# New durations in the table of a build-time instruction scheduler, and a price for a change of rows on TensorE

## The chip, the cores and the metric

The kernel runs on one core of one Trainium2 chip. The metric is the device time of one execution in microseconds, the median of several runs. A core has a matrix engine (TensorE, PE in the profile, with its weight loads shown apart as PEld), VectorE (DVE), ScalarE (ACT), GpSimd (POOL) and the DMA queues, here issued by SyncE (SP). Each engine works through its own instructions in the order in which the program lists them; across engines they wait on semaphores.

## What is computed

Four transformer layers on 256 tokens of width 1024, all in float32, cut here to their skeleton:

```python
for l in range(2):                       # first block
    x = x + 0.5 * rmsnorm(swiglu(rmsnorm(x, g), w_gate, w_up, w_down), g_post)   # ffn1
    x = x + rmsnorm(token_mixing(rmsnorm(x, g), ...), g_post)                    # mix
    x = x + 0.5 * rmsnorm(swiglu(rmsnorm(x, g), ...), g_post)                    # ffn2
for l in range(2):                       # second block
    x = x + merged(nsa_attention, gated_linear_attention, memory_attention) @ w_out   # hyb
    x = x + square(relu(rmsnorm(x, g) @ w_up)) @ w_down                              # mlp
```

`token_mixing` runs three kinds of attention over 16 heads. `merged` gates and adds three branches: sparse attention (8 heads of 64, in pairs), gated linear attention (4 heads, "gla") and attention into a memory of 256 tokens (4 heads).

## The kernel before

**Main stream.** All weights (some 640 blocks of 128 x 1024 float32, called halves) are read in the order of use. Each is split into a high and a low part in TensorE's faster float32 format: ACT copies the high part (`splits`), DVE subtracts to get the low part (`lows`), and where DVE falls behind, POOL does that subtraction in four pieces of 256 columns (`pooled`). TensorE multiplies each half with all 256 tokens, mostly with 256 or 512 moving columns a matmul (`ws_mm`, `ts_mm`, `ts_bank`). At the end of a stage `finish` multiplies the last chunks, and for each of the two tiles of tokens `residual`, `norm` and `turn_half` make the next stage's input on ACT, DVE and POOL; `turn_half` transposes it on TensorE. In the gaps after the first block's stages TensorE has other products to make (`fill`: keys and values of the memory); `ws_first` starts the next stage with the tile that is ready.

**Background.** The attentions run as tasks beside the main stream. The order of the matmuls inside a task is written out: `scores` and `nsa_pair` give for each segment of scores one matmul over all 128 rows of the array (both parts of one operand stacked) and then one over the 64 rows of the head; `gla` gives for each head a group of some ten products over 64 rows, of 16 to 256 columns, whose operands three multiplications on POOL have prepared (of 128, 256 and 512 columns); before its transposes `nsa_pair` scales probabilities with six instructions on POOL for each of two groups of heads.

**The order.** The program is made by a list scheduler that runs when the kernel is built (`Sched`). Every instruction is an `Op` with a planned duration: `mm` and `tr` set it for TensorE, `Engine` for the other engines. `Sched.run` takes at each step the instruction that can start first by the planner's clocks (`when`), with small biases by priority, and issues it; `matmul` and `stream` advance TensorE's clock. Nothing else of the plan reaches the chip: it sets the order on each engine and which buffer each task gets. Priority 0 (`CHAIN`) is the work at the end of a stage, 2 and 4 are background, 9 is the main stream. A background matmul is held back on purpose:

```python
if t.op.eng == "pe" and 0 < p < 9:
    w = max(w, t.op.rdy + self.SLACK)        # SLACK = 1.17 us
k = (w + t.bias, p, t.seq)                   # main stream: bias 0.05
```

The planner's prices before, in microseconds: a matmul 0.4167e-3 a column plus 0.002; a transpose of 128 columns 0.1067 plus 0.002; a two-operand instruction on POOL 2.07e-3 a column plus 0.157; on POOL a scaling by a column (`tensor_scalar`) 0.85e-3 a column plus 0.24.

Of the kernel before, what the change touches and what calls it, by code (L numbers as in the profile page):

```python
# [45 lines left out]
# ---------------------------------------------------------------- weights  # L46
# The main stream reads the weights in the order of use, in "halves":
# [128, 1024] float32, what one step multiplies with all 256 tokens.

def ws_half(w, c0):  # L50
    """Columns c0:c0+128 of a [1024, n] matrix: [128 p, 8 k, 128 c]."""
    return w[:, c0:c0 + 128].reshape(8, 128, 128).transpose(1, 0, 2).reshape(128, 1024)


def ts_halves(w, cols, per=2):
    """Columns of a [1024, n] matrix, per row chunks of 128 in a half: [128 p, per, n]."""
    a = w[:, cols]
    n = a.shape[1]
    a = a.reshape(8 // per, per, 128, n).transpose(0, 2, 1, 3).reshape(8 // per, 128, per * n)
    if per * n < 1024:  # L60
        a = np.concatenate([a, np.zeros((8 // per, 128, 1024 - per * n), np.float32)], -1)
    return list(a)
# [59 lines left out]
def merge_order(b):  # L122
    """Gates (None, j) and branch halves (i, None) of a branch."""
    if b == 0:
        return [(None, j) for j in range(8)] + [(i, None) for i in range(4)]
    return [u for i in range(4) for u in ((None, 2 * i), (None, 2 * i + 1), (i, None))]
# [56 lines left out]
# ---------------------------------------------------------------- constants of the shapes  # L183
# [9 lines left out]
def constants():  # L193
# [25 lines left out]
    # decay sums: E[tok] = sum over a range of tokens, as columns of 0 or -1/16  # L219
# [10 lines left out]
    # order F, 1, 2, 4, B, 64, 32, 16, 8  # L230

    # predicates for A^T[j, i] of the levels that are computed whole: i = j, and 1, 2, 4, 8
# [13 lines left out]
def prepare(inp, stages):  # L246
# [15 lines left out]
    # block two: per-partition columns of gains, and rows that are broadcast  # L262
# [13 lines left out]
# ---------------------------------------------------------------- the kernel  # L276

class Slots:
    """Tiles that are handed out and returned; a task yields (slots) or (slots, n) to get some."""
# [23 lines left out]
class Op:  # L303
    """One instruction, not yet issued."""
    __slots__ = ("eng", "call", "args", "kw", "cost", "tail", "outs", "ins", "tab", "rdy", "stamp", "fn", "load",
                 "passes", "cols", "dep", "name")

    def __init__(self, eng, call, args, kw, cost, outs, ins, tail=0.0, tab=None, fn=None, load=0.0, passes=1, cols=0.0):
# [5 lines left out]
        self.fn = fn  # L314


def region(a):
    """(name, in PSUM, partitions, elements of a partition) that an operand covers; whole banks of PSUM."""
# [28 lines left out]
class Engine:  # L347
    """Makes the instructions of one engine."""
# [4 lines left out]
    def __getattr__(self, fn):  # L353
# [3 lines left out]
        def make(*args, **kw):  # L357
# [22 lines left out]
            else:  # L380
                k, b = 2.07, 0.157
# [25 lines left out]
class Sched:  # L407
    """Lists the instructions of all tasks in one order: the one that can start first by the engines'
    clocks is issued first. A task is a generator of instructions (Op), of conditions to wait for
    (a function) and of requests for tiles (Slots, or (Slots, n))."""  # L410


    def __init__(self):
# [3 lines left out]
        self.table = None  # L417
# [12 lines left out]
    def step(self, t):  # L430
        """Runs a task up to its next instruction, or until it has to wait."""
# [54 lines left out]
    def stream(self, s, cost, cols):  # L486
        """The end of a matmul that starts at s: the array runs at half its clock in a period that follows
        one of little activity."""
# [9 lines left out]

    def matmul(self, op):
        w = self.ready(op)  # L500
        for i in range(op.passes):
            ld = max(self.loader, w) + op.load
            self.loader = max(ld, self.t.get("pe", 0.0) + 0.002)
# [5 lines left out]
    def when(self, op):  # L509
        c = self.t.get(op.eng, 0.0)  # L510
        if op.eng == "pe":
            return max(c, max(self.loader, self.ready(op)) + op.load)
# [96 lines left out]
class Prog:  # L609
# [41 lines left out]
    # ---- small helpers  # L651
# [10 lines left out]
    def mm(self, out, lhsT, rhs, start, stop, **kw):  # L662
# [3 lines left out]
                  wide * 0.4167e-3 * n, [out], [lhsT, rhs], fn="mm", load=0.836e-3 * m, passes=wide,  # L666
                  cols=wide * n * rhs.shape[0] / 128)

    def tr(self, out, in_, k=128):
        i = self.ident[:k, :k]  # L670
        return Op("pe", self.nc.tensor.transpose, (out, in_, i), {}, 0.8333e-3 * k, [out], [in_, i], fn="tr", load=0.107, cols=2 * k)

    def mm3(self, out, l, r, start=True, stop=True):
        """Product of split operands: l(hl), r(hl) give the parts."""
# [6 lines left out]
    def gain(self, ap):  # L681
        """A gain [1024] on every partition, in a scratch tile."""
# [8 lines left out]
    def hl_gain(self, H, L, src, g):  # L691
        """Split of src * g, g a column or a number."""
# [3 lines left out]
    def chunk(self, src):  # L696
        """A split [128, 256] operand for the main stream."""
# [4 lines left out]
    # ---- weights: loaded and split ahead of the main stream  # L702
# [45 lines left out]
    def pooled(self, low):  # L748
        """Takes what the vector engine falls behind with."""
# [22 lines left out]
    # ---- norms  # L772
    def rstd(self, st, a, b, n):
        """(sum of columns a and b of st + n eps)^-0.5, in place of a."""
# [5 lines left out]
    def norm(self, t, x, Gn, dst, st):  # L780
        """dst[:, k, t, hl, :] = rms(x) * gain of token tile t, transposed and split. Gn: the gain times 32."""
# [31 lines left out]
    # ---- matrix products of the main stream  # L813
    def ws_mm(self, p, w, act, nk=8, off=0, parts=1):
        """Weights stationary. One part: [128 columns, 256]; two, which value() adds: [128 columns, t, hl, 128]."""
# [19 lines left out]
    def ws_first(self, n, done):  # L835
        """The first n products of a stage: those of the first tile of tokens ahead of the others."""
# [23 lines left out]
    def ws_unit(self, parts=1):  # L860
        """One product of the main stream: (result, where it goes back to, parts)."""
# [6 lines left out]
    def value(self, pr):  # L868
        """A product as one [128, 256] operand, and the tile that holds it if there is one."""
# [19 lines left out]
    def ts_bank(self, y, w, c, t, first, last, **kw):  # L889
        """y += tokens of tile t times a chunk w(hl) of weights; c: [128, t, hl, 128]."""  # L890
# [3 lines left out]
    def ts_mm(self, y, w, c, t, first):  # L894
        """y [128, 2, 512] += tokens of tile t times w [128, 1024]."""
# [4 lines left out]
    def ts_group(self, width, split=False):  # L900
        """All tokens times a group of columns: a pair of banks, tokens of a tile in each."""
# [22 lines left out]
    # ---- the end of a stage: the last chunks, residual, next norm  # L924
    def gains(self, post, after):
        """The gains for the end of a stage: that of its result, times 32 and the residual's factor, and the next one's, times 32."""
# [9 lines left out]
    def finish(self, chunks, names, ys, post, after, fills):  # L936
        """The last chunks (by name) of a stage; ys: the banks of the tiles of tokens."""
# [63 lines left out]
    def give_gain(self, name):  # L1001
        """Both tiles of tokens are through with a gain."""
# [5 lines left out]
    # ---- memory: keys and values of both layers, in the gaps between the stages  # L1008
# [16 lines left out]
    def fill(self, f):  # L1025
        """256 columns of the memory's keys (f%4 < 2) or values."""
# [22 lines left out]
    def mem_keys(self, l, c, p, y):  # L1049
        """Normed keys of two heads, transposed: memk[:, head, memory token]."""  # L1050
# [17 lines left out]
    # ---- the feed-forward networks  # L1068
# [71 lines left out]
    # ---- token mixing of block one  # L1140
# [15 lines left out]
    def table(self, name):  # L1156
        """The functions of the next stage, once this one's are done with."""
# [3 lines left out]
    def qk_post(self, l, it, pr, qk):  # L1161
# [9 lines left out]
        else:  # L1171
            # of each of two heads: queries with the high parts on its rows and the low ones on the others;
            # keys with the high parts on all rows, and the low ones on its own
# [55 lines left out]
    def scores(self, s, q, k, rows, stacked, strict=False):  # L1229
        """s: a bank [128 q, (q1: 256 keys | q0: 256 keys)] for each of two row groups."""  # L1230
# [14 lines left out]
    def smax(self, Pt, s, biases):  # L1245
        """Exponentials of biased scores of two maps: P [128, 2, 384], and their sums in st[:, :, 2:4]."""
# [15 lines left out]
    def pv_t(self, Tt, Ps):  # L1262
        """Transposed probabilities [128 k, n, (k0: q0 q1 | k1: q1)] of maps [128 q, (q1: k0 k1 | q0: k0)]."""
# [14 lines left out]
    def pv_mm(self, p, T, col):  # L1278
        """o^T [128 = 2 heads x 64, 256 tokens]; V columns col, col+64."""
# [38 lines left out]
    def att_b(self, j, q, k):  # L1318
# [33 lines left out]
        # r = (mean of the squares of a head + eps)^-0.5 on every partition of the head  # L1352
# [42 lines left out]
    # ---- block two  # L1395
# [31 lines left out]
    def rope_tables(self):  # L1427
        nc, a = self.nc, self.a
        # cos and sin of position * frequency: [128, 3, 8] (two token tiles, block ends)
# [24 lines left out]
    def again(self, tag, shape, dt=FT):  # L1454
        """A new tile in the place of the last one of a tag."""
# [7 lines left out]
    def rope(self, x, cos, sin, shape):  # L1463
        """Rotates the first 16 of the last axis of x [.., 64] in place."""
# [18 lines left out]
    def head_norm(self, x, p, nt, nh, d, gs, times=1.0):  # L1483
        """x [p, nt, nh, d] in place: rms over d, gains (view of x, gain) or none, times a factor."""
# [59 lines left out]
    def cmp_post(self, v, pr):  # L1544
        """The windows of compressed keys or values: 2 x 16 positions of each, split."""
# [55 lines left out]
    def hyb(self, l, after, fills):  # L1601
# [7 lines left out]
        # gates, low-rank gate, memory queries, gla values  # L1609
# [27 lines left out]
        # merge  # L1637
# [39 lines left out]
    # ---- memory attention  # L1677
# [60 lines left out]
    # ---- gated linear attention  # L1738
    def gla_gate(self, l):
        """sp = -log sigmoid of the gates, per token, split: [128 tokens, hl, t, 256]."""  # L1740
# [27 lines left out]
    def gla(self):  # L1768
        nc, gq, gr, gv = self.nc, self.gq, self.gr, self.tB
        och = self.och[1] = {}  # L1770
        for half in range(2):
# [6 lines left out]
            for t in range(2):  # L1778
# [14 lines left out]
                # slots: t0: 1 2 4 B | 64 32 16 8, t1: F 1 2 4 | 64 32 16 8  # L1793
# [36 lines left out]
            # o [tokens, dv] of both heads, normed, then transposed  # L1830
# [41 lines left out]
    # ---- nsa: queries, keys, then the three branches  # L1872
    def nsa_qk(self):
# [17 lines left out]
        # of a row group g: rows 64g.. the high parts, the other rows the low parts  # L1891
# [31 lines left out]
    def split_v(self):  # L1923
        yield lambda: ("o", 1) in self.done
        # a token tile, kind: 64 values of the first group, zeros, 64 of the second
# [7 lines left out]
    def keys(self, src, view):  # L1933
        """The high parts of the keys of a row group on all rows, and the low parts on its own."""
# [261 lines left out]
```

## Time and profile before

| What | Value |
|---|---|
| median of 3 runs | 2043.14 us (2041.13 to 2045.71) |
| span of the profiled execution, first to last instruction | 2040.8 us |
| its own time beside the span | not recorded; the three runs lie 0.3 to 4.9 us above the span |
| mean granted TensorE clock over the span | 0.994 of full speed |
| TensorE: busy in matmuls | 1995.6 us, 98% of the span |
| VectorE, ScalarE, GpSimd busy | 70%, 59%, 13% |

The span is what the profile measured between the first and the last instruction of one execution; start and end of the program lie around it. All instructions of this kernel are recorded at one line, so groups are told apart by tiles and shapes. A matmul's recorded duration overlaps with that of the next, so that the distance of starts tells more than the duration.

### The profile page before, as it was taken

The page shows a single profiled execution, that of the slowest core. Times are in us where ns is not written, and L with a number is a line of the kernel's source. Part 1 is how long each engine was busy: PE and PEld are TensorE (multiplying, and loading weights), DVE is VectorE, ACT ScalarE, POOL GpSimd, SP SyncE. Part 2 cuts the span into 40 slices and gives each one's busy share as a digit, 9 for nine tenths or more (in the row PEclk, how much of TensorE's full clock was granted, in tenths as well). Part 3 has the DMA queues.
Part 4 walks back from the last instruction along what each step waited for, and adds up shares of the span by engine and source line. Part 5 has one row for each costly group of instructions (what it writes and reads, how often), then busy time and mean ns, then how long its engine had stood idle before and what let it go on. Part 6 is the DMA issues. An engine that isn't in the chain of part 4 may idle for free. (4 is left out here: it accounts for less than half of the span.)

```text
span 2040.8 us, 31877 instructions
## 1 busy us (share of the span) xinstructions
PE 1995.6 (98%) x11942; PEld 1732.3 (85%) x11942; DVE 1424.7 (70%) x2525; ACT 1205.0 (59%) x2328; POOL 267.7 (13%) x311
## 2 busy tenths in 40 slices
PE   8999999999999999999999999999999999999999
PEld 7888777888888887788889888998888978898887
DVE  6666887666776678776668777666667787667665
ACT  6655775655565568665556656655555656655553
POOL 1000302000200030020003132310001232411000
PEclk9999999999999999999999999999999999999999
DMA  6655344655665644455565544355565544335553
GB/s 218 222 192 199 117 152 146 215 193 188 208 198 192 206 156 135 167 176 190 187 206 193 173 146 135 102 167 183 192 198 189 165 148 142 114 130 191 188 194 124
DMA packets 100561, 353.77 MB, mean 173 GB/s; under 512 B 12435, under 2 KB 13493, under 8 KB 100406
## 3 DMA queue, kind: packets, MB, share of 16 engines
q1 hardware_dynamic: 100406, 351.74, 52.2%
q8 instruction: 93, 1.52, 0.3%
q14 instruction: 62, 0.51, 0.1%
HBM read 350.64 MB, written 1.05 MB: 172 GB/s over the span
## 5 line engine op out<-in xcount | busy, mean ns | idle before, releaser
L546 PE MATMUL m<-hT,hl 128*128 128x256 f32 (+1 forms) x5856 | 976.4, 322 | 7.7 <-DVE hT L546 7.0
L546 PEld LDWEIGHTS m<-hT,hl 128*128 128x128 f32 x5856 | 853.6, 189 | 104.1 <-DVE hT L546 9.6
L546 ACT CAST hl<-raw 128x1024 fp32r<-128x1024 f32 (+1 forms) x690 | 671.4, 982 | 380.3 <-PE b L546 141.3
L546 DVE TENSOR_TENSOR hl<-raw,hl 128x1024 fp32r<-128x1024 f32 (+1 forms) x641 | 755.5, 1184 | 200.1 <-ACT hl L546 193.1
L546 PE MATMUL b<-hl,chunk 128*128 128x512 f32 x2208 | 517.0, 390 | 0.0
L546 PEld LDWEIGHTS b<-hl,chunk 128*128 128x128 f32 x2208 | 408.9, 188 | 81.8 <-issue 0.7
L546 DVE TENSOR_TENSOR mid<-m,lo 128x256 f32<-128x256 f32 x256 | 108.5, 424 | 221.8 <-ACT lo L546 221.3
L546 PE MATMUL b<-hl,hT 128*128 128x512 f32 (+2 forms) x672 | 149.4, 371 | 0.5 <-DVE hT L546 0.5
L546 ACT CAST chunk<-mid 128x256 fp32r<-128x256 f32 x152 | 61.7, 406 | 120.8 <-DVE mid L546 120.4
L546 POOL TENSOR_SCALAR scr<-scr 128x1024 f32<-128x1024 f32 x17 | 21.1, 1239 | 834.9 <-DMA scr<-ffn_post_g 451.6
L546 PEld LDWEIGHTS b<-hl,hT 128*128 128x128 f32 x672 | 115.9, 188 | 16.6 <-DVE hT L546 0.8
L546 POOL TENSOR_TENSOR hl<-raw,hl 128x256 fp32r<-128x256 f32 x104 | 103.0, 1017 | 192.0 <-ACT hl L546 155.1
L546 ACT COPY lo<-m 128x256 f32<-128x256 f32 x256 | 95.0, 371 | 23.8 <-PE m L546 22.7
L546 PE MATMUL b<-ident,scr 128*128 128x128 f32 (+2 forms) x458 | 78.3, 284 | 17.8 <-DVE scr L546 14.0
L546 PE MATMUL m<-chunk,hl 128*128 128x256 f32 x576 | 82.4, 292 | 0.0
L546 PEld LDWEIGHTS b<-ident,scr 128*128 128x128 f32 (+2 forms) x458 | 54.3, 143 | 33.0 <-DVE scr L546 20.3
L546 PEld LDWEIGHTS m<-chunk,hl 128*128 128x128 f32 x576 | 74.3, 195 | 3.0 <-ACT scr L546 0.7
L546 ACT ACTIVATE scr<-scr,sts 128x16 f32<-128x16 f32 (+2 forms) x152 | 62.8, 415 | 9.4 <-DVE sts L546 9.1
L546 DVE TENSOR_TENSOR chunk<-mid,chunk 128x256 fp32r<-128x256 f32 x152 | 65.3, 430 | 2.3 <-ACT chunk L546 2.0
L546 POOL TENSOR_SCALAR scr<-scr,sts 128x128 f32<-128x128 f32 (+2 forms) x96 | 55.9, 602 | 79.3 <-DVE sts L546 52.1
L546 ACT COPY scr<-b 16x16 f32<-16x16 f32 (+6 forms) x148 | 35.4, 239 | 41.2 <-PE b L546 33.5
L546 ACT ACTIVATE mid<-mid 128x256 f32<-128x256 f32 x88 | 36.7, 417 | 34.1 <-DVE mid L546 34.1
(204 smaller groups left out, 1622.4 us busy)
## 6 DMA issues: line engine op xcount, KB each, us to landing
raw<-w SPq DMA_DIRECT2D x636, 512.0 KB, 3.4
scr<-mem SPq DMA_DIRECT2D x4, 512.0 KB, 6.2
scr<-ffn_post_g SPq DMA_DIRECT2D x4, 512.0 KB, 5.0
bias<-bias SPq DMA_DIRECT2D x6, 256.0 KB, 3.6
scr<-ffn_pre_g SPq DMA_DIRECT2D x3, 512.0 KB, 5.9
scr<-mem_norm SPq DMA_DIRECT2D x2, 512.0 KB, 4.9
scr<-mix_pre_g SPq DMA_DIRECT2D x2, 512.0 KB, 4.2
bias<-alibi SPq DMA_DIRECT2D x4, 256.0 KB, 4.3
```

Source lines behind the costliest of these rows:

```text
L546: r = op.call(*op.args, **op.kw) if op.call is not None else None
```

## The change

TensorE's prices become 0.4227e-3 a column plus 0.0105 for each matmul, 0.011 more for each weight load, and 0.098 for a transpose. The two-operand price of POOL becomes 3.1e-3 a column. Each matmul now has a mode, the number of rows of the array that it uses; in the plan a change of mode costs 0.195 us. While TensorE is in a mode of fewer than 128 rows, `when` moves every matmul of another mode 0.195 us later, so that one of the same mode goes first if it is ready by then. Transposes of 64 rows or fewer take whatever mode is current. SLACK, the biases, the prices of ACT and DVE, of the powers and the scalings on POOL, and the instructions themselves stay. The diff also removes comments and docstrings, left out here.

```diff
+                 mode=None):
...
-        self.fn = fn
+        self.fn, self.mode = fn, mode
...
-                k, b = 2.07, 0.157
+                k, b = 3.1, 0.157
...
-        self.table = None
+        self.table = self.mode = None
...
+    SWITCH = 0.195
+    STEP = 0.0105
+
     def matmul(self, op):
         w = self.ready(op)
+        if op.mode != self.mode:
+            if self.mode is not None:
+                w = max(w, self.t.get("pe", 0.0) + self.SWITCH - op.load)
+            self.mode = op.mode
         for i in range(op.passes):
             ld = max(self.loader, w) + op.load
-            self.loader = max(ld, self.t.get("pe", 0.0) + 0.002)
+            self.loader = max(ld, self.t.get("pe", 0.0) + self.STEP)
...
         if op.eng == "pe":
-            return max(c, max(self.loader, self.ready(op)) + op.load)
+            back = self.SWITCH if self.mode not in (None, 128) and op.mode != self.mode else 0.0
+            return max(c + back, max(self.loader, self.ready(op)) + op.load)
...
-                  wide * 0.4167e-3 * n, [out], [lhsT, rhs], fn="mm", load=0.836e-3 * m, passes=wide,
-                  cols=wide * n * rhs.shape[0] / 128)
+                  wide * 0.4227e-3 * n, [out], [lhsT, rhs], fn="mm", load=0.836e-3 * m + 0.011, passes=wide,
+                  cols=wide * n * rhs.shape[0] / 128, mode=rhs.shape[0])
...
-        return Op("pe", self.nc.tensor.transpose, (out, in_, i), {}, 0.8333e-3 * k, [out], [in_, i], fn="tr", load=0.107, cols=2 * k)
+        return Op("pe", self.nc.tensor.transpose, (out, in_, i), {}, 0.098, [out], [in_, i], fn="tr", load=0.109, cols=2 * k,
+                  mode=128 if k > 64 else self.sch.mode)
```

## Rows read from the trace of the kernel before

**Rows 1.** The page: the span, and each engine's busy time.
```profile
span 2040.8 us, 31877 instructions
PE 1995.6 (98%) x11942; PEld 1732.3 (85%) x11942; DVE 1424.7 (70%) x2525; ACT 1205.0 (59%) x2328; POOL 267.7 (13%) x311
```

**Rows 2.** TensorE's waits: for whom, us in total, times, longest us.
```profile
PE b L546 <- DVE scr L546: 14.0, 21, 1.7
PE b L546 <- POOL scr L546: 10.7, 6, 3.5
PE m L546 <- DVE hT L546: 7.0, 10, 1.0
...
PE b L546 <- DVE chunk L546: 1.0, 1, 1.0
```

**Rows 3.** Groups of matmuls by shape: count, busy us, mean ns, idle before.
```profile
L546 PE MATMUL m<-hT,hl 128*128 128x256 f32 x3936 | 552.0, 286 | 7.7 <-DVE hT L546 7.0 <-DVE scr L546 0.5
L546 PE MATMUL b<-hl,chunk 128*128 128x512 f32 x2208 | 517.0, 390 | 0.0
...
L546 PE MATMUL b<-kst,qk 64*128 64x256 f32 x48 | 18.3, 381 | 0.0
...
L546 PE MATMUL b<-tA,hlq 64*128 64x272 f32 x32 | 12.4, 388 | 0.0
...
L546 PE MATMUL b<-tA,hlq 64*128 64x256 f32 x16 | 6.1, 381 | 0.0
```

**Rows 4.** TensorE in order of time, 204 to 208 us: start, us, count.
```profile
204.29 3.35 PE L546 MATMUL m<-hl,hmem 128*128 128x256 f32 x27
207.48 0.60 PE L546 MATMUL b<-ident,scr 128*128 128x128 f32 x4
```

**Rows 5.** TensorE in order of time, 288 to 291 us: eight matmuls of scores.
```profile
287.99 2.47 PE L546 MATMUL b<-kst,qk 128*128 128x256 f32 x8
290.39 2.84 PE L546 MATMUL m<-hT,hl 128*128 128x512 f32 x15
```

**Rows 6.** TensorE in order of time, 1644 to 1646 us: products of gla.
```profile
1644.53 0.97 PE L546 MATMUL b<-scr,scr 64*128 64x128 f32 x16
1645.43 0.33 PE L546 MATMUL m<-hl,rawhl 128*62 128x256 f32 x1
1645.69 0.48 PE L546 MATMUL b<-scr 64*128 64x128 f32 x2
```

**Rows 7.** TensorE in order of time, around 1206 us, the wait in brackets.
```profile
1205.91 1.50 PE L546 MATMUL b<-scr,scr 64*128 64x128 f32 x16 [3.52 <-POOL scr L546]
```

**Rows 8.** GpSimd in order of time, around 1200 us.
```profile
1198.18 7.68 POOL L546 TENSOR_TENSOR scr<-scr,tC 128x128 f32<-128x128 f32 x3
```

**Rows 9.** Stretches: length; PE, PEld, DVE, ACT, POOL busy (count); clock, DMA share, GB/s.
```profile
1114.30:1119.00 4.70, 4.64 (x40) 4.44 (x39) 4.67 (x4) 3.23 (x5) 4.67 (x4) 1.00 0.39 112
1198.20:1205.80 7.60, 4.19 (x28) 3.26 (x26) 6.49 (x8) 1.83 (x3) 7.60 (x4) 0.97 0.40 135
1205.90:1207.90 2.00, 1.99 (x18) 1.36 (x18) 0.00 (x0) 0.37 (x3) 2.00 (x3) 0.50 0.01 2
```

**Rows 10.** The same view, the stretch after the wait of Rows 7.
```profile
1206.00:1213.10 7.10, 7.10 (x47) 6.08 (x48) 2.68 (x12) 1.72 (x10) 1.91 (x3) 0.56 0.41 148
```

**Rows 11.** GpSimd's scalings of one pair of heads in order of time.
```profile
1265.04 7.24 POOL L546 TENSOR_SCALAR scr<-scr,sts 128x128 f32<-128x128 f32 x12 [7.63 <-DVE sts L546]
```

**Rows 12.** TensorE in order of time: two transposes of nsa_pair that wait for GpSimd.
```profile
1269.06 0.29 PE L546 MATMUL b<-ident,scr 128*48 128x128 f32 x1 [1.44 <-POOL scr L546]
...
1315.47 0.29 PE L546 MATMUL b<-ident,scr 128*48 128x128 f32 x1 [0.43 <-POOL scr L546]
```

**Rows 13.** TensorE in order of time, the end of the first mix stage.
```profile
543.68 0.66 PE L546 MATMUL b<-ident,scr 128*128 128x128 f32 x4 [0.70 <-DVE scr L546]
...
549.45 0.65 PE L546 MATMUL b<-ident,scr 128*128 128x128 f32 x4 [0.23 <-DVE scr L546]
549.86 2.37 PE L546 MATMUL m<-hl,hmem 128*128 128x256 f32 x18
```

More of the change, by code (lines that the diff above doesn't have):

```diff
@@ L305, with __init__ @@
     __slots__ = ("eng", "call", "args", "kw", "cost", "tail", "outs", "ins", "tab", "rdy", "stamp", "fn", "load",
-                 "passes", "cols", "dep", "name")
-    def __init__(self, eng, call, args, kw, cost, outs, ins, tail=0.0, tab=None, fn=None, load=0.0, passes=1, cols=0.0):
+                 "passes", "cols", "dep", "name", "mode")
+    def __init__(self, eng, call, args, kw, cost, outs, ins, tail=0.0, tab=None, fn=None, load=0.0, passes=1, cols=0.0,
+                 mode=None):
         self.eng, self.call, self.args, self.kw, self.cost, self.tail, self.tab = eng, call, args, kw, cost, tail, tab
```

## The prediction

> **What bounds the kernel now.** I read the page first: TensorE is in matmuls for 1995.6 of 2040.8 us, while DVE is at 70% and ACT at 59% [rows 1]. So only TensorE's own time counts, and a new order of the same instructions can change three things in it: waits of TensorE for other engines, the cost of going from one number of rows to another, and stretches at the lower clock that follow an idle TensorE.
>
> The list of TensorE's waits gives the first. The rows shown sum to 32.7 us, the two largest being transposes that wait for DVE (14.0 us in 21 pieces) and matmuls that wait for POOL (10.7 us in 6) [rows 2]. That is 1.6% of the span, and most of it lies at ends of stages, where a chain of norms has to run before there is new work. No order can win much more than 1%; a bad one can lose more. The view by shape shows what the waits are not: the main stream's 3936 matmuls of 256 columns idled 7.7 us in all, the 2208 of 512 columns not at all [rows 3]. The reader should see that planner and chip agree well already where it counts: hardly anything in mid-stage waits.
>
> **TensorE's new price.** 27 matmuls of 256 columns start between 204.29 and 207.48, so each takes 3.19/27 = 0.118 us [rows 4]. The planner took 256 x 0.4167e-3 + 0.002 = 0.1087 and now takes 256 x 0.4227e-3 + 0.0105 = 0.1187, 9% more and right; a transpose stays (0.1087 to 0.1085). Correct as it is, this moves background work forward in TensorE's order: the planner places a dependent matmul when its operand is ready by its clock, plus SLACK, and fills the time until then with main matmuls. A time T that was filled with T/0.1087 matmuls is now filled with T/0.1187. On the chip the old filling lasted T x 0.118/0.1087 = 1.086 T, the new one 0.994 T. The old error was a hidden reserve of 9%; it is gone wherever the other engines are still priced too short. The work of the main stream does not shrink, so nothing is gained by being earlier, except where background work ends last, and rows 2 show no such place.
>
> **Background chains.** SLACK of 1.17 us remains for each. A chain as long as the 4.24 us that the plan has for the scalings of a pair (below) loses 0.092 x (4.24 + 1.17) = 0.5 us of cover; I take that for all of them, an estimate. 12 tasks of block one and, in block two, 8 of memory, 8 of gla and 8 of pairs are 36 chains; with two such steps each, all exposed, it is 36 us. But only one short wait of this kind is in the rows (1.0 us, for chunk [rows 2]). I take +1.5, with 0 and +12 (a third exposed) as ends.
>
> **Pairs of heads.** Here POOL is priced too short, and the change leaves that price alone. Twelve scalings take 7.24 us [rows 11]; by the front's prices they are 4 x (0.349 + 0.458 + 0.254) = 4.24. Transposes behind them wait 1.44 and 0.43 us [rows 12], and with the second layer the same again: 2 x 1.87 = 3.74 of POOL's 10.7. The planner fills 4.24 + 1.17 = 5.41 us: before with 49.8 matmuls, 5.87 us on the chip, now with 45.6, 5.38 us. Each wait grows by 0.49; four make +2.0. Hidden neighbours (eight pairs in all) could double it, a luckier place of DVE's work could take it away: 0 to +4.
>
> **End of a stage.** The transposes of `turn_half` have priority 0 and no SLACK. Where TensorE runs out of other work anyway, placing them earlier only moves the wait. After mix there is work left: behind the fourth of four such waits 18 matmuls of the memory follow at once [rows 13]. These four run from 543.68 to 549.45, so about 6 us of filling lose 0.5. Two layers: +1.0, from 0 to +2.
>
> **Changes of rows.** Eight matmuls of scores, alternately 128 and 64 rows, take 290.39 - 287.99 = 2.40 us, 0.300 each where 0.118 is usual [rows 4, 5]: a round trip costs 2 x 0.182 = 0.364. The 64-row matmuls of scores (48) and of the pairs (32 + 16) [rows 3] each stand behind a 128-row one in their own task's written order, and `when` only holds back what follows a small matmul, so these 96 round trips stay. Left are gla's groups. One is parted by a single main matmul [rows 6]; the main stream's weights were narrower (62 columns), so it could start a little before the group's next. The new 0.195 ends that. I take four such places, 4 x 0.364 = -1.5; if each of gla's 16 groups lost one round trip, -5.8; nothing if other operands are late, 0.
>
> **POOL's new price.** Each layer has one long wait of gla for POOL, 3.52 us [rows 7]; (10.7 - 3.74)/2 = 3.5 for the mean. In the 7.1 us from 1206.0 the granted clock is 0.56, nearly all at the lower of TensorE's two levels (1.2 of 2.4 GHz) [rows 10]: 7.1 x 0.44 = 3.1 us lost. Before it, TensorE had idled for those 3.5 us. Both layers could give back 2 x (3.5 + 3.1) = 13.2 us. But the three multiplications that it waits for took 7.68 us [rows 8]; the plan had 0.42 + 0.69 + 1.22 = 2.33 and now has 0.55 + 0.95 + 1.74 = 3.25. So 0.92 of a shortage of 5.35 is mended, less 0.092 x (2.33 + 1.17) = 0.32 for the lost cover: -0.6 a layer, -1.2 in all, from -13.2 to +0.6.
>
> The rows also show why no price per column can be right. Four pieces of 256 columns took 4.67 us, 1.17 each, while DVE was busy in the same stretch; three took 2.00, 0.67 each, while DVE did nothing [rows 9]. The old price was 0.687, the new one is 0.951: between the two, and true of neither. In gla's case DVE was busy for 6.49 of 7.60 us [rows 9].
>
> The Trainium skill (GPSIMD Engine Reference, section 1, Specifications) states that POOL's SBUF interfaces are shared with VectorE, with contention when a DVE instruction has two SBUF inputs. The trace agrees (1.17 against 0.67). By that rule alone the new price helps nothing where DVE is in the way, and this term would be +0.6 instead of -1.2, the sum +3.6.
>
> **Sum.** +1.5 + 2.0 + 1.0 - 1.5 - 1.2 = +1.8 us. The execution of the profile would go from a span of 2040.8 to 2042.6; on the median of 2043.14, 2.3 above that span, it is 2044.9, so 2045. Faster or slower by 0.2%, 4.1 us, is about what a measurement here can tell from no change.
>
> **Rivals.** *No change that counts* (2039 to 2047, my forecast): the terms nearly cancel, for a kernel that hardly waits in mid-stage.
>
> *Faster: the long waits of gla go.* The plan with true matmul prices lays DVE's and ACT's work beside TensorE's as it will be, so that the subtractions on DVE may no longer fall on POOL's three multiplications; or their operands are just ordered later. Then 13.2 us come back and the other terms but this one stay at +3.0: 2043.1 - 13.2 + 3.0 = 2033; half of it gives 2039. For it: the largest single waits sit there. Against it: 4.4 us of the shortage stay in the plan. It decides once the wait is short enough that the clock stays up, for then 3.1 us go with it.
>
> *Slower: the wait of the pairs grows into one like gla's.* The plan is 7.24 - 4.24 = 3.0 us short there, and only 1.17 of SLACK and the old reserve stood against it. If the 1.44 us become 3.5 and the clock falls behind it as in rows 10, each layer pays 2.1 + 3.1: +10.4. The other terms without these two waits are 1.8 - 1.0 = +0.8, so 2043.1 + 10.4 + 0.8 = 2054; with the waits alone and no lower clock, 2048. For it: POOL's scalings keep their price. Against it: buffers and DVE also set when a pair starts, and they are priced as before. It decides from about 3.5 us of wait.
>
> **How the numbers follow.** Forecast 0.35, faster 0.32, slower 0.33; the same are the chances of the three classes, since the cases are bounded at 0.2%. The predicted time is the first case's, 2045. Its own range is 2039 to 2047. Eight times in ten the time should lie between 2031 (the faster case and two microseconds of luck elsewhere) and 2058 (the slower case with a few exposed chains); both signs hold most of the chance, so it can't be narrower.
>
> **What would show it.** Matmuls of 256 columns stay at 0.118. TensorE's waits for POOL by tile: below 4 us in all means the faster case, above 14 the slower. Waits for DVE above 14.0, and new small waits of `scores`' and pairs' transposes, would show the lost reserve. Runs of 64-row matmuls in gla should be parted less often, those of scores as before. Stretches below full clock should lie where they lay, behind gla's waits. I am wrong in kind if the main stream itself begins to wait (for split weights), or if DVE and ACT, ordered anew, leave the chain at the ends of stages much later or earlier than now.

## The result and the profile after

The changed kernel takes 2065.81 us (median of 4 runs, 2064.26 to 2067.78), the kernel before beside it 2044.24 (4 runs). The ratio is 1.0108, 95% interval 1.0093 to 1.0122: slower by 22 us, above the range of 2031 to 2058.

The profile after: the line of the core (span, mean granted clock), the page's busy times, and three groups by shape.

```profile
core 0: 2062.5 us, clock 0.990
...
PE 2008.8 (97%) x11942; PEld 1740.3 (84%) x11942; DVE 1422.0 (69%) x2538; ACT 1208.1 (59%) x2328; POOL 219.9 (11%) x271
...
L555 PE MATMUL m<-hT,hl 128*128 128x256 f32 x3936 | 549.4, 286 | 5.0 <-DVE hT L555 5.0
...
L555 PE MATMUL m<-chunk,hl 128*128 128x256 f32 x576 | 83.5, 297 | 7.0 <-ACT scr L555 6.8
...
L555 POOL TENSOR_TENSOR scr<-scr,tC 128x512 f32<-128x512 f32 x8 | 10.3, 1282 | 0.0
```

Against [rows 1, 3] the matmuls are the same in number, and the 3936 of them are no slower. New is the second group: the main-stream matmuls over the branches' results (`chunk`) in block two's merge stand behind 7.0 us of idle TensorE, nearly all of it a wait for ACT. In the kernel before that group had none:

```profile
L546 PE MATMUL m<-chunk,hl 128*128 128x256 f32 x576 | 82.4, 292 | 0.0
...
L546 POOL TENSOR_TENSOR scr<-scr,tC 128x512 f32<-128x512 f32 x8 | 18.9, 2360 | 0.0
```

TensorE's waits after (for whom: us in total, times, longest), against [rows 2]:

```profile
PE b L555 <- DVE scr L555: 20.5, 20, 5.2
PE m L555 <- ACT scr L555: 6.8, 5, 2.2
PE m L555 <- DVE hT L555: 5.0, 7, 1.0
PE m L555 <- DVE mid L555: 3.8, 4, 1.3
...
PE b L555 <- POOL scr L555: 1.5, 1, 1.5
```

The long waits for POOL are gone (10.7 to 1.5), as in the prediction's faster case. Transposes wait 6.5 us more for DVE, but 5.2 of their 20.5 us are one wait at the start of the program, where the kernel before had waited 3.5 us for ACT instead:

```profile
21.58 1.97 PE L555 MATMUL b<-ident,scr 128*128 128x128 f32 x8 [5.21 <-DVE scr L555]
```

The main stream itself (tiles `m`) waits for ACT's `scr` and for DVE's `mid`, 10.6 us in two rows that did not exist before. The prediction had named a waiting main stream as the sign of being wrong in kind, though it looked for it at the split weights.

The largest wait of the main stream, as TensorE and ACT show it in order of time:

```profile
1220.57 0.63 PE L555 MATMUL b<-dec,sp 128*128 128x512 f32 x2
1223.45 1.70 PE L555 MATMUL m<-chunk,hl 128*128 128x256 f32 x12 [2.25 <-ACT scr L555]
```

```profile
1219.14 1.27 ACT L555 COPY scr<-b 16x16 f32<-16x16 f32 x7
1222.48 0.42 ACT L555 COPY vcmp<-b 15x64 f32<-15x64 f32 x2 [2.06 <-DVE vcmp L555]
1222.92 0.47 ACT L555 ACTIVATE scr<-m,cols 128x256 f32<-128x256 f32 x1
```

In this kernel ACT stands idle for 2.06 us in front of a background copy (into `vcmp`) whose turn has come but whose tile DVE has not cleared yet. Behind it in ACT's queue is the reading of `m` by a gate of the merge (1222.92), and the main stream's next matmul starts 0.53 us after that begins. DVE's list shows why the clearing is late: two subtractions of 1024 columns (2.35 us) stand ahead of it in the queue.

```profile
1219.71 2.35 DVE L555 TENSOR_TENSOR hl<-raw,hl 128x1024 fp32r<-128x1024 f32 x2
1221.98 0.28 DVE L555 COPY_PREDICATED scr<-pred,b 128x128 f32<-128x128 uint8 x1
1222.23 0.17 DVE L555 MEMSET vcmp<- 48x128 f32 x1
```

What follows for the clock, by stretches (length; busy PE, PEld, DVE, ACT, POOL; clock, DMA share, GB/s):

```profile
1216.00:1223.40 7.40, 5.20 (x52) 4.34 (x50) 7.40 (x15) 3.50 (x14) 3.24 (x3) 1.00 0.46 146
...
1226.80:1230.60 3.80, 2.70 (x24) 2.50 (x22) 3.69 (x7) 2.12 (x4) 1.96 (x2) 1.00 0.43 138
1230.60:1237.50 6.90, 6.90 (x45) 6.08 (x46) 6.57 (x16) 3.38 (x11) 2.54 (x1) 0.68 0.59 212
```

DVE is busy for all 7.40 us of the first stretch. TensorE idles 2.2 us there and 1.1 in the second, and then runs 6.9 us at a mean of 0.68, so for most of it at 1.2 GHz of 2.4.

**One table for all that follows.** Columns: the profiled span; what weight loads waited for DVE, ACT and POOL, from the list of TensorE's waits, summed per engine; the mean granted clock; and lateness against the kernel before at the end of block one and over block two. The main stream's matmuls come in the same order in every kernel, so the start of the n-th can be compared; block two begins where the n-th is the first of `hyb`. Lateness is counted from the trace, in us, from the start of the first of these matmuls on. Each row is one execution. That of p_pool is the fastest of its five runs: their spans go from 2020.9 to 2035.3 us, with 2029.8 in the middle.

| Kernel | span | DVE | ACT | POOL | clock | block one | block two |
|---|---|---|---|---|---|---|---|
| before | 2040.8 | 36.3 | 5.1 | 12.0 | 0.994 | 0 | 0 |
| changed | 2062.5 | 52.3 | 14.9 | 2.4 | 0.990 | +11.3 | +10.9 |
| p_matmul | 2065.5 | 42.7 | 10.0 | 14.9 | 0.989 | +11.9 | +13.6 |
| p_mode | 2045.5 | 39.3 | 10.7 | 5.4 | 0.992 | +4.5 | +0.5 |
| p_pool | 2020.9 | 34.5 | 4.4 | 1.1 | 1.000 | -6.4 | -13.0 |
| p_poolmode | 2058.4 | 35.9 | 18.0 | 12.3 | 0.988 | -0.7 | +18.2 |
| a_scale109 | 2043.3 | 34.6 | 10.2 | 13.6 | 0.993 | -0.6 | +2.3 |
| p_matmul_scale109 | 2045.1 | 38.3 | 4.0 | 6.1 | 0.990 | +1.8 | +2.3 |
| p_poolhold | 2021.0 | 32.9 | 5.8 | 0.4 | 0.997 | -5.5 | -13.9 |
| p_poolcharge | 2029.6 | 31.4 | 10.5 | 5.7 | 0.997 | -3.6 | -7.6 |
| a_hold_scale109 | 2031.2 | 33.7 | 6.7 | 2.8 | 0.997 | +2.0 | -11.9 |

The 21.7 us of span come roughly out of it: DVE +16.0, ACT +9.8, POOL -9.6; the clock (1 - 0.990) x 2062.5 - (1 - 0.994) x 2040.8 = +8.4; and 289 changes of rows along TensorE's list instead of 301, 12 x 0.182 = -2.2. Together +22.4. That it comes so near is in part luck: the same sum gives -26 for p_pool, whose span is 19.9 us shorter, and TensorE's idle time itself (span less busy) grows by only 8.5 us, from 45.2 to 53.7.

### The profile page after: what moved, and what is told of

Same layout as the page of the kernel before. It is cut to its first block, busy times and chain, and to the rows that moved or that the text cites. A ratio compares the mean times of both kernels' runs of the same rounds, so it can differ in the third digit from the quotient of the medians.

```text
span 2062.5 us, 31860 instructions
## 1 busy us (share of the span) xinstructions
PE 2008.8 (97%) x11942; PEld 1740.3 (84%) x11942; DVE 1422.0 (69%) x2538; ACT 1208.1 (59%) x2328; POOL 219.9 (11%) x271
## 5 line engine op out<-in xcount | busy, mean ns | idle before, releaser
L555 PE MATMUL b<-ident,scr 128*128 128x128 f32 (+3 forms) x458 | 80.5, 289 | 22.4 <-DVE scr L555 19.4
L555 PEld LDWEIGHTS b<-ident,scr 128*128 128x128 f32 (+3 forms) x458 | 53.3, 144 | 40.7 <-DVE scr L555 28.5
L555 POOL TENSOR_TENSOR hl<-raw,hl 128x256 fp32r<-128x256 f32 x64 | 66.5, 1065 | 43.9 <-ACT hl L555 43.9
L555 POOL TENSOR_SCALAR scr<-scr,sts 128x128 f32<-128x128 f32 (+1 forms) x96 | 45.7, 498 | 66.0 <-DVE sts L555 52.5
```

The source lines that it names most:

```text
L555: r = op.call(*op.args, **op.kw) if op.call is not None else None
```

## The experiments

Theories: *lost reserve* (the plan's ratio of TensorE's price to the other engines' is what counts; the old 9% was cover), *SLACK* (only SLACK is too short now), *luck* (any new order costs that much), and the change's three parts each by itself. Names beginning with a_ start from the changed kernel, b_ from the kernel before, p_ from one or two parts of the change.

**The three parts, each alone.** Each is the kernel before with one part of the change; p_mode has the lines with `SWITCH` and `mode` as the change has them.

```diff
 # p_matmul (and the same for the load and the transpose)
-            self.loader = max(ld, self.t.get("pe", 0.0) + 0.002)
+            self.loader = max(ld, self.t.get("pe", 0.0) + self.STEP)
...
-                  wide * 0.4167e-3 * n, [out], [lhsT, rhs], fn="mm", load=0.836e-3 * m, passes=wide,
+                  wide * 0.4227e-3 * n, [out], [lhsT, rhs], fn="mm", load=0.836e-3 * m + 0.011, passes=wide,
 # p_pool
-                k, b = 2.07, 0.157
+                k, b = 3.1, 0.157
```

p_matmul: 

> Only the prices of matmuls, weight loads and transposes are the new ones; a change of rows costs nothing in the plan, POOL keeps 2.07e-3 a column. Theory (lost reserve: with true matmul prices the plan lays dependent matmuls too early for DVE and ACT): this part alone carries the loss, 2058 to 2068 us, with DVE's and ACT's waits above 30 us. Rival (lottery: the order before happens to be a good one, and any new order costs about 1%): also 2055 to 2070, no different. Rival (the price of rows does it): 2040 to 2048.

p_mode: 

> Only the modes: 0.195 us for a change of rows in the plan and the holding back of other rows. Lost reserve: 2039 to 2048, since only places with 64-row matmuls lose cover and some round trips vanish. Lottery: 2055 to 2070, because the order changes from the first attention on. Price of rows does it: 2058 to 2068.

p_pool: 

> Only POOL's two-operand price, 3.1e-3 a column. Lost reserve: 2038 to 2046, the waits for POOL a little shorter than 10.7 us. Lottery: 2055 to 2070, for the share of splits that POOL takes changes early and with it the whole order.

Measured: p_matmul 2067.22 us (1.011, 1.0095 to 1.0125), p_mode 2045.62 (1.0005, 0.9995 to 1.0014), p_pool 2031.59 (0.9928, 0.9902 to 0.9953). TensorE's true price alone costs as much as the whole change, POOL's price alone gains 0.72%, 15 us, and the prices of the change of rows alone do nothing that can be measured. By medians POOL's price gains 12.7 us; its runs spread from 2022.7 to 2037.1, and both theories had put it higher. The 2067 of p_matmul lies in the bands of lost reserve and of luck alike and does not part them. The waits of p_pool and p_matmul:

```profile
PE b L550 <- DVE scr L550: 10.8, 12, 2.0
...
PE b L550 <- POOL scr L550: 0.7, 2, 0.3
```

```profile
PE b L550 <- DVE scr L550: 18.2, 22, 1.7
PE b L550 <- POOL scr L550: 13.6, 5, 6.9
...
PE m L550 <- ACT scr L550: 0.9, 1, 0.9
PE m L550 <- DVE mid L550: 0.7, 1, 0.7
```

With POOL's old price TensorE's price lengthens gla's wait to 6.9 us; with POOL's new one and TensorE's old, it vanishes. The main stream's waits for ACT's `scr` and DVE's `mid` are 1.6 us in p_matmul, against 10.6 in the changed kernel: TensorE's price alone does not make them.

**Two parts, and the changed kernel with more SLACK.** p_poolmode is the changed kernel with TensorE's old prices; the others change one line.

```diff
-    SLACK = 1.17
+    SLACK = 1.70    # a_slack17; 2.20 in a_slack22
```

p_poolmode: 

> The changed kernel without the new prices of matmuls, weight loads and transposes: modes and POOL's price alone. Lost reserve: 2026 to 2042 us, the gain of POOL's price with the nothing of the modes. Lottery: anywhere from 2025 to 2070.

a_slack17: 

> The changed kernel with SLACK 1.70 in place of 1.17, which gives a background chain of 4 to 5 us about the cover that it had before. Lost reserve: 2045 to 2056, background waits for DVE and ACT much shorter, while those at ends of stages (priority 0, no SLACK) and of the main stream stay. Lottery: 2058 to 2072, no relation to SLACK.

a_slack22: 

> The changed kernel with SLACK 2.20. If the loss sits in background chains alone, it goes on falling from the 2058 of 1.70, to 2045 to 2053. If the rest sits in what has no SLACK (ends of stages, the main stream's own waits for buffers and operands), it stays at 2054 to 2062. Lottery: anywhere.

Measured: p_poolmode 2060.3 us (1.0081, 1.0066 to 1.0096), a_slack17 2058.15 (1.007, 1.0053 to 1.0087), a_slack22 2062.53 (1.009, 1.006 to 1.012). SLACK gives back a third at 1.70, to just above the band of lost reserve and the lower edge of luck's, and nothing clear at 2.20, where two runs lie at 2056 to 2058 and two at 2067 to 2069. So it is no cure; that `turn_half` and the main stream have no SLACK would fit, but no run tests it. And two parts that were harmless or better alone lose 0.8% together, 17 us, with TensorE's old prices, where the theory of the lost reserve had expected a gain. The table puts all of that into block two (+18.2), where the main stream waits for ACT as in the changed kernel:

```profile
PEld b L555 <- POOL scr L555: 11.9, 6, 3.1
...
PEld m L555 <- ACT scr L555: 7.3, 2, 3.8
```

So the changed kernel's 22 us are not TensorE's price and nothing else: without that price 17 us are lost, and with it only 5.5 more. In block one the parts can be told apart: p_matmul and the changed kernel are 11 to 12 us late there, p_poolmode is not.

**The ratio restored.** All prices but TensorE's, all latencies and SLACK by 9% up (not the biases and ACT's table load), so that TensorE's true price of 256 columns stands to them as the old one did. a_scale109 does it in the changed kernel, p_matmul_scale109 in p_matmul.

```diff
-            return Op(e, real, args, kw, cost, outs, ins, tab=tab, fn=fn)
+            return Op(e, real, args, kw, 1.09 * cost, outs, ins, tab=tab, fn=fn)
...
-    SLACK = 1.17
+    SLACK = 1.275
```

a_scale109: 

> The changed kernel, with every price of ACT, DVE, POOL and the transfers, every latency between engines and SLACK times 1.09, so that they stand to TensorE's new price as they stood to its old one. Lost reserve (only the ratio of TensorE's price to the others counts): back to what the kernel without the new matmul prices does, 2028 to 2045 us. If a plan with true matmul prices is bad for another reason, such as the order that it gives the main stream: 2055 to 2070.

p_matmul_scale109: 

> TensorE's new price alone (no held rows, POOL's old price), and every price of ACT, DVE, POOL and the DMAs, every latency and SLACK raised by 9%, so that the ratio of TensorE's price to all others is that of the kernel before. Lost reserve (the ratio is what counts): the time returns to the kernel before, 2039 to 2048, with waits for DVE near 36 us and none of the main stream for its own buffers. Rival (TensorE's price itself does it, by making the planner count its time rightly): it stays near the 2067 of that price alone. Rival (every new order costs something by luck): 2050 to 2060.

Measured: 2042.95 us (0.9998, 0.9989 to 1.0008) and 2042.89 (0.9999, 0.9989 to 1.0008). Both are back at the time of the kernel before. TensorE's waits in a_scale109:

```profile
PE b L555 <- POOL scr L555: 11.8, 7, 2.9
PE b L555 <- DVE scr L555: 8.9, 11, 1.4
PE m L555 <- DVE hT L555: 6.2, 8, 1.1
...
PE m L555 <- DVE mid L555: 0.8, 2, 0.4
```

The row for DVE's `scr` falls from 20.5 to 8.9, and no `m <- ACT scr` is left. In p_matmul_scale109 that row stays at 20.6 (4.2 of it one wait at 31.98), so by itself it is no measure of the loss.

p_matmul_scale109 is the clean case: TensorE's price alone, and the whole loss gone. So it is not that the plan counts TensorE's time rightly, but that it then counts the others too short beside it. a_scale109 says less. In its ratios it is nearly p_poolmode, which took 2060.3 us, 17 more; what differs is smaller things that did not rise by 9% (the charge for a change of rows, the biases, transposes and matmuls of 512 columns; the new price of those of 128 columns rose by more). That the ratio is all that counts is therefore not shown for the plan with the charge in it.

**Luck, and the kernel before with less SLACK.** SLACK 1.15 changes nothing that matters and gives another order: counted from the traces, 9 to 16 in 100 background matmuls stand at another place among the main stream's. The change and each of its parts move 22 to 26.

```diff
-    SLACK = 1.17
+    SLACK = 1.15    # a_, b_, p_pool_ and p_poolmode_slack115; 0.67 in b_slack067
```

b_slack067: 

> The kernel before with SLACK 0.67 in place of 1.17 and all its old prices: the reserve of background chains is cut by 0.5 us, about what the new matmul prices cut. Lost reserve in the background: 2049 to 2062 us, with new short waits for DVE and ACT. If the loss sits in work without SLACK: 2040 to 2048.

b_slack115: 

> The kernel before with SLACK 1.15 in place of 1.17: a change with no sense of its own that moves some instructions. It measures how far the time strays with the order. Lost reserve, with an order that matters little by itself: 2036 to 2050. Lottery with the order before a lucky one: 2050 to 2065.

a_slack115: 

> The changed kernel with SLACK 1.15. Lost reserve: stays slow, 2056 to 2074. Lottery: anywhere from 2030 to 2070, and under 2050 would say that the changed kernel had an unlucky order.

p_pool_slack115: 

> POOL's price alone, with SLACK 1.15. If its gain (2031.6) comes from pricing POOL nearer the truth, it stays: 2025 to 2038. If it was luck: 2038 to 2062.

p_poolmode_slack115: 

> POOL's price and the modes, with SLACK 1.15. If the 2060 of the two together is a coincidence of one long wait in each hyb stage: 2030 to 2050. If the two prices work against each other by their nature: 2055 to 2066.

Measured: b_slack067 2050.5 us (1.0036, 1.0024 to 1.0047), b_slack115 2043.98 (0.9996, 0.9987 to 1.0006), a_slack115 2062.24 (1.0092, 1.0076 to 1.0108), p_pool_slack115 2030.37 (0.9926, 0.9909 to 0.9944), p_poolmode_slack115 2062.24 (1.0085, 1.0062 to 1.0108). The neutral new order, one for each, moves the time by at most 3.6 us. It is a smaller shuffle than the change's own, but p_mode and p_matmul_scale109 move as many matmuls as the change (22 and 25 in 100) and take the time of the kernel before. So luck is a poor explanation of the loss, of POOL's gain and of the loss of the pair. And half a microsecond less reserve costs the kernel before 0.36%, 7 us, a third of what the price did: the direction is that of the lost reserve.

**POOL's price in a plan with the ratio kept.** p_matmul_scale109 with POOL's new price.

```diff
-                k, b = 2.07, 0.157
+                k, b = 3.1, 0.157    # times 1.09, as all prices but TensorE's
```

p_mmpool_scale109: 

> TensorE's new price and POOL's new price, no held rows, and everything but TensorE's prices raised by 9%: the kernel before in its ratios, but for POOL, whose piece of 256 columns counts 1.04 us beside TensorE's true 0.118. If the ratio is what counts and POOL's price was worth 12 us by itself, this gives 2028 to 2036, as POOL's new price alone did. If POOL's gain hung on one lucky order, it is lost here: 2041 to 2050.

Measured: 2036.64 us (0.9958, 0.9942 to 0.9975), between the two bands. The price gains 0.4% there, 8 us, a little over half of what it gains alone; the two intervals overlap.

**Which half of the change of rows.** Both with POOL's new price and TensorE's old ones.

```diff
 # p_poolcharge: the plan's clock is charged, nothing is held back
-            return max(c + back, max(self.loader, self.ready(op)) + op.load)
+            return max(c, max(self.loader, self.ready(op)) + op.load)
 # p_poolhold: held back, but not charged
-                w = max(w, self.t.get("pe", 0.0) + self.SWITCH - op.load)
+                pass
```

p_poolcharge: 

> POOL's new price, and of the change of rows only the charge of 0.195 us in the plan's clock; a large matmul is not held back behind a small one. TensorE's old prices. Theory A (the charge makes the plan's TensorE later than it is, so work for the second block's tasks comes earlier in the order and takes buffers): near the 2060 of both halves. Theory B (the holding back does it: main matmuls that would have covered POOL are kept out while a group of 64 rows is open): near the 2032 of POOL's price alone.

p_poolhold: 

> POOL's new price, and of the change of rows only the holding back of a large matmul behind a small one; no charge in the plan's clock. TensorE's old prices. Theory B (holding back does it): near the 2060 of both halves. Theory A (the charge does it): near 2032. If both this and the charge alone stay near 2032, the two together are needed; if both lose, the gain of POOL's price hangs on the one order that it happened to give in the second block.

Measured: p_poolcharge 2031.17 us (0.994, 0.9925 to 0.9955), p_poolhold 2020.82 (0.9885, 0.987 to 0.99). Neither half loses; holding back alone is the fastest so far, faster than either theory had it. What it looks like at the place of [rows 7], where TensorE goes from gla's second product to its groups:

```profile
1193.38 0.70 PE L555 MATMUL b<-scr,tC 64*128 64x256 f32 x2
1194.00 1.22 PE L555 MATMUL m<-chunk,hl 128*128 128x256 f32 x8
1195.15 0.71 PE L555 MATMUL b<-scr,scr 64*128 64x128 f32 x4
1195.79 1.70 PE L555 MATMUL m<-chunk,hl 128*128 128x256 f32 x12
1197.42 0.97 PE L555 MATMUL b<-scr,scr 64*128 64x128 f32 x16
```

```profile
1192.57 4.77 POOL L555 TENSOR_TENSOR scr<-scr,tC 128x128 f32<-128x128 f32 x3
```

No matmul waits. POOL's three multiplications take 4.77 us where they took 7.68 [rows 8], and they start 0.8 us ahead of the products over `tC`. In p_poolmode, with the charge added, they take 6.97 us, there are 3 main matmuls instead of 8 behind those products, and TensorE waits:

```profile
1199.81 0.70 PE L555 MATMUL b<-scr,tC 64*128 64x256 f32 x2
1200.44 0.62 PE L555 MATMUL m<-chunk,hl 128*128 128x256 f32 x3
1203.94 0.71 PE L555 MATMUL b<-scr,scr 64*128 64x128 f32 x4 [2.89 <-POOL scr L555]
```

```profile
1198.15 6.97 POOL L555 TENSOR_TENSOR scr<-scr,tC 128x128 f32<-128x128 f32 x3
```

**Holding back, checked, and put together with the ratio.**

```diff
 # p_poolhold_slack115: p_poolhold with
+    SLACK = 1.15
 # a_hold_scale109: a_scale109 with the charge taken out, as in p_poolhold
```

p_poolhold_slack115: 

> POOL's new price with the holding back alone, which gave 2020.8, and SLACK 1.15 in place of 1.17: another order of the same plan. If the 22 us are a property of the two edits, the time stays within 2016 to 2028. If it was one lucky order, it goes to 2030 or above.

a_hold_scale109: 

> The changed kernel without the charge of 0.195 in the plan's clock (the holding back stays), and everything but TensorE's prices raised by 9%. If the ratio of the prices carries the loss and the charge beside the holding back eats POOL's gain, both cures add up: 2018 to 2030. If the charge is not what eats it in this setting, it stays at the 2043 of the same plan with the charge; in between, 2034 to 2040, only half of it is the charge.

Measured: 2019.31 us (0.9876, 0.9858 to 0.9894) and 2031.2 (0.993, 0.9912 to 0.9948). The first is the fastest kernel of the study, 25 us under the kernel before, and the gain holds in another order. The second lies just above the band in which both cures would add up, and 0.7%, 14 us, below the same plan with the charge (0.993 against 0.9998): also with the ratio restored, it is the charge beside the holding back that eats POOL's gain. In the table POOL's waits fall from 13.6 to 2.8 between the two.

## Why the prediction was wrong

**TensorE's price.** The step that failed is *Background chains*. Its mechanism is the one that the runs bear out: filling counted with a true price covers less time, and with all other prices 9% up the loss is gone (p_matmul_scale109). Its size was off by an order: +1.5, at most +12 (with pairs and ends of stages, +4.5, at most +18), against +22 (1.1% of 2044, p_matmul). I sized the chains by the one short wait that the rows before showed, but what lost its cover there showed no wait at all, because the reserve had hidden it. By the table, p_matmul's weight loads wait 6.4 us more for DVE, 4.9 for ACT and 2.9 for POOL (gla's longest wait grows from 3.5 to 6.9), and the clock costs 10.5 us more. For the clock behind many small waits my sum had no term. It said that the low stretches would stay behind gla's waits, though in the kernel before already one lay elsewhere (last section). Chains with priority 0 and no SLACK stand at the start and the ends of stages; block one, which has no gla, is 11.3 us late in the changed kernel and 11.9 in p_matmul.

**That the terms add up.** The second step that failed is the sum itself: it took *Changes of rows* and *POOL's new price* as two terms of -2.7 together. With TensorE's old prices the two edits cost 17 us (p_poolmode, 2060.3 against 2043.0), and TensorE's prices on top only 5.5. The changed kernel has two causes of its loss, each enough for most of it. The waits of the main stream belong to the pair: for ACT's `scr` they are 6.9 us in p_poolmode and 0.9 in p_matmul.

```profile
PE m L555 <- ACT scr L555: 6.9, 2, 3.6
```

The prediction asked only whether the main stream has its weights. Its tiles `m` come free when ACT or DVE has read them, and those readers can stand in a queue behind background work whose turn comes too early (2.25 us at 1223); the sum had no term for that.

**POOL's price.** The mechanism was right, its size not: -1.2 forecast, -15 measured alone (-10 to -20 by the interval, -12.7 by medians), about the lower bound of -13.2. I worked the term out of gla's one bad case, where 0.92 of 5.35 us is mended. The price is used at every such instruction. The rows of the kernel before have 104 pieces of weights at a mean of 1.017 us: the old price, 0.687, was a third short, the new one, 0.951, is nearly right on the mean. That it is true of no single case need not matter for an order; which of the many instructions brought the gain no run shows.

```profile
L546 POOL TENSOR_TENSOR hl<-raw,hl 128x256 fp32r<-128x256 f32 x104 | 103.0, 1017 | 192.0 <-ACT hl L546 155.1 <-DVE scr L546 36.8
```

The rule of the Trainium skill (GPSIMD Engine Reference, section 1, Specifications) that POOL's SBUF interfaces are shared with VectorE, with contention when a DVE instruction has two SBUF inputs, was no reason for +0.6. The multiplication of 512 columns that gla waits for took 5.58 us in the kernel before; in p_poolhold, with some of DVE's products still beside it, it takes 2.68, and in the changed kernel 1.28. A new order moves such work apart or together, and the sum had held it fixed. The 1.17 us that the prediction read as the price beside a busy DVE is a mean of four pieces of 0.74 to 1.71.

**Changes of rows.** -1.5 forecast, -2.2 by the count of 289 for 301, and nothing in the time: p_mode is at 1.0005, and its row of the table has new waits beside what it saves (ACT +5.6, DVE +3.0, POOL -6.6). The sum left out that a price in the plan's clock moves everything behind it. Holding back without the charge gains about 9 us beside POOL's price (0.9885 against 0.9928).

**Pairs and ends of stages.** That the waits of pairs would grow (+2.0), and the slower rival with them, was wrong: after the change one wait for POOL's `scr` is left, 1.5 us. I took the scalings' 7.24 us for fixed, 3 us more than the plan has; in the new order they got shorter, from 0.60 to 0.50 us on the mean:

```profile
L546 POOL TENSOR_SCALAR scr<-scr,sts 128x128 f32<-128x128 f32 (+2 forms) x96 | 55.9, 602 | 79.3 <-DVE sts L546 52.1
L555 POOL TENSOR_SCALAR scr<-scr,sts 128x128 f32<-128x128 f32 (+1 forms) x96 | 45.7, 498 | 66.0 <-DVE sts L555 52.5
```

Ends of stages were forecast at +1.0. Transposes' waits for DVE grow from 14.0 to 18.2 in p_matmul; in the changed kernel they grow to 20.5, or 15.3 without the one wait at the start of the program.

**The faster rival** came true in its condition, gla's waits gone, and gave nothing, because its "other terms stay at +3.0" did not hold: they were about 31 (22 plus the 9 us that POOL's waits fell). The order that took gla's waits away made others in the merge.

**Open.** Why charge and holding back, each harmless with POOL's price, lose 28 to 40 us together in block two. The rows show the waits (gla's for POOL, the merge's for ACT, the clock behind both) and that a neutral order doesn't remove them, not which decision of the planner makes them. That the charge makes the plan's TensorE later, as its price did, would fit, but the charge without the holding back loses nothing. Why a_scale109 loses nothing where p_poolmode, with nearly the same ratios, loses 17 us is open with it.

## What to carry to other kernels

A list scheduler goes by how its prices stand to each other, not by their truth: correct one engine's price alone and the error of the others, which it had hidden, can come out, as in p_matmul. Before such an edit, ask of each queue what stands behind a background instruction in it, and count as exposed all that the old error covered, not only what waits today. Change one price at a time, and test each with a neutral shift of another constant: here the whole was 1.1% slower, and POOL's price with half of the change of rows 1.2% faster.

## What the runs showed of the hardware

The same POOL multiplication of 128x512 float32 has a mean of 2.36, 1.64 and 1.28 us in the kernel before, p_poolhold and the changed kernel, but the mean hides two kinds. In the kernel before six of the eight took 1.28 to 1.29 us and two, those that gla waited for, 5.58. DVE was busy beside both kinds; what it was busy with differs. These are the stretches of one of each, and DVE's main instructions in them:

```profile
1146.66:1147.94 1.28, 1.28 (x6) 0.78 (x6) 1.19 (x3) 0.00 (x0) 1.28 (x2) 1.00 0.34 138
1200.28:1205.86 5.58, 2.11 (x15) 1.65 (x13) 4.45 (x7) 1.36 (x2) 5.58 (x3) 0.96 0.27 93
```

```profile
1146.21 1.67 DVE L546 TENSOR_TENSOR scr<-m,pe 64x240 f32<-64x240 f32 x4
1200.52 1.27 DVE L546 TENSOR_TENSOR tA<-tA,grow 128x512 f32<-128x512 f32 x2
1202.06 1.21 DVE L546 TENSOR_TENSOR hl<-raw,hl 128x1024 fp32r<-128x1024 f32 x1
```

DVE was busy for 1.19 of the 1.28 us, with sums over a tile `m` of PSUM, and POOL's multiplication was no longer for it. Beside the long one DVE was busy for 4.45 us, mostly with products and subtractions of two SBUF tiles, and the multiplication took 4.30 us more. So what falls beside what changed POOL's durations here.

And the clock fell behind waits shorter than the 3.5 us of gla: in the changed kernel 2.25 and 1.10 us of idle TensorE at 1223 and 1230 stood ahead of a stretch at 0.68. In the kernel before it did so too, behind waits of 0.98 and 0.71 us between two stages:

```profile
1377.71 0.74 PE L546 MATMUL m<-hT,hl 128*128 128x256 f32 x4 [0.98 <-DVE hT L546]
1379.17 1.43 PE L546 MATMUL m<-hT,hl 128*128 128x256 f32 x6 [0.71 <-DVE hT L546]
```

```profile
1379.30:1383.30 4.00, 3.67 (x19) 3.38 (x20) 3.19 (x5) 0.81 (x3) 0.78 (x2) 0.57 0.77 265
```
